# Two padding tiles ahead of and behind the normed activations of a hybrid decoder layer

## The chip, the core and the metric

The kernel runs on one core of a Trainium2 chip. The metric is the device time of one execution in microseconds (us). The time before is the median of two runs. A separate view, the profile, shows one execution instruction by instruction.

## The reference

One decoder layer on 512 tokens of width 1024, in float32, cut to what matters here:

```python
def swiglu_ffn(x, w_gate, w_up, w_down):
    return (jax.nn.silu(x @ w_gate) * (x @ w_up)) @ w_down

x = x + 0.5 * swiglu_ffn(rmsnorm(x, g1), w_gate1, w_up1, w_down1)   # 1024 -> 2816 -> 1024
x = x + mixer(rmsnorm(x, g2))       # h @ w_in (2048 columns), two causal mixers, @ w_out
x = x + 0.5 * swiglu_ffn(rmsnorm(x, g3), w_gate2, w_up2, w_down2)
y = rmsnorm(x, g4)
```

The mixer splits h @ w_in into a convolution branch (gated, depthwise convolution of width 31, layer norm, swish) and a recurrent branch (convolution of width 4, gates, a scan over the tokens, multiplied by a GELU branch).

## The kernel before

**Products in two parts.** Every large product is made from float32r operands that are split in a high and a low part: hi*hi + lo*hi + hi*lo, so three matmuls for one product. Weights come from HBM in slabs of 512 KB (`raw`). ScalarE copies the high part into `hl[:, 0]`, and VectorE (in some stages GpSimd) writes the low part into `hl[:, 1]`. `raw` has 3 buffers and `hl` has 5.

**Two kinds of matmul streams.** They differ in which operand stands still in the array and which one moves through it.

- `mm_feat` (line 194): the weights `hl` stand still, 128 columns at a time, and the normed and transposed activations `h_hi` and `h_lo` move, 512 tokens or 256 tokens at a time. It makes gate and up of both feed-forward blocks (PSUM tiles `pgate`, `pup`) and the input projection of the mixer (`pz`). 24 matmuls make one unit.
- `mm_tok` (lines 329 to 331): the inner activations (`act`, or `uhi`, `ulo`, `yhi`, `ylo` of the mixer) stand still and the weights `hl` move, always 512 columns. It makes the down products and the output projection (PSUM tiles `pd`, `pdl`).

```python
seq = [(0, h_hi), (0, h_lo), (1, h_hi)]
for s, (a, h) in enumerate(seq):
    for k in range(KT):                                  # mm_feat, KT = 8
        PE.matmul(ps, w[:, a, k, :], h[:, k, t0:t0 + n], ...)

PE.matmul(ps, ahi, whi, start=first, stop=False)          # mm_tok
PE.matmul(ps, ahi, wlo, start=False, stop=False)
PE.matmul(ps, alo, whi, start=False, stop=last)
```

The first operand after `ps` is the stationary one, the second is the moving one. Each matmul comes with a weight load of its own (PEld in the profile).

**Order of the stages**, with the times at which they stand in the profile: first norm and two early pairs of units on 256 tokens (12 to 39 us), gate and up on 512 tokens (39 to 129), first part of down (129 to 183), gate and up (183 to 318), down (318 to 364), mixer with the recurrences, the convolutions, the output projection and the first units of the second feed-forward block (364 to 609), the rest of gate and up (609 to 684, mostly on 256 tokens), down (684 to 739), gate and up (739 to 874), down and the final norm (874 to 946).

**Tiles in SBUF.** The pool `cp` holds one buffer for each persistent tile, in the order in which `const` is called (line 76). Its first tile begins 128 bytes past a multiple of 512 in each partition. The four tiles `xt0` to `xt3` take 4096 bytes each, and `h_hi` and `h_lo` 16384 bytes each. A 128-column slice of float32r is 512 bytes and a 512-column slice 2048 bytes, so all slices of one tile that the matmuls read begin at the same offset modulo 512. In the built program before, these offsets are:

| tile | role | offset modulo 512 |
|---|---|---|
| `h_hi`, `h_lo` | moving in `mm_feat` | 128 |
| `hl` (5 buffers) | stationary in `mm_feat`, moving in `mm_tok` | 480 |
| `act`, `uhi`, `ulo`, `yhi`, `ylo` (19 shared buffers) | stationary in `mm_tok` | 480 |
| `raw` (3 buffers) | source of the split | 480 |

Of the kernel before, what the change touches and what calls it, by code (L numbers as in the profile page):

```python
# [13 lines left out]
P = 128  # L14
# [44 lines left out]
def layer_kernel(ctx: ExitStack, tc, x, gains, w_g1, w_u1, w_d1a, w_d1b, w_in,  # L59
# [16 lines left out]
    def const(shape, name, dt=F32):  # L76
        return cp.tile(shape, dt, name=name, tag=name)

# [1 line left out]
    xt = [const([P, D], f"xt{t}") for t in range(4)]  # L80
    h_hi = const([P, KT, T], "h_hi", F32R)
    h_lo = const([P, KT, T], "h_lo", F32R)
    ident = const([P, P], "ident")
    ones = const([P, P], "ones")
    neghalf = const([P, 1], "neghalf")
# [16 lines left out]
        nc.sync.dma_start(g, gains[i:i + 1, :].broadcast_to([P, D]))  # L102
        return g

# [1 line left out]
    clock = {"pe": 0.0, "dve": 0.0, "pool": 0.0}  # L106
    chains, convs, done = [], [], {}

    def dve(us):
        clock["dve"] = max(clock["dve"], clock["pe"] - 3.0) + us  # L110

    # slabs are loaded, then split into two parts of float32r
    def slab_load(st, src):
        st["raw"] = wp.tile([P, D], F32, name=nm("raw"), tag="raw", bufs=RAW_BUFS)
        nc.sync.dma_start(st["raw"], src)
# [69 lines left out]
            if evac is not None:  # L185
                evac()

# [1 line left out]
    def mm_feat(ps, hl, t0, n):  # L189
        w = hl.rearrange("p s (k f) -> p s k f", k=KT)  # L190
        seq = [(0, h_hi), (0, h_lo), (1, h_hi)]
        for s, (a, h) in enumerate(seq):
            for k in range(KT):
                PE.matmul(ps, w[:, a, k, :], h[:, k, t0:t0 + n],  # L194
                          start=(s == 0 and k == 0), stop=(s == 2 and k == KT - 1))
# [5 lines left out]
            tc.keep_in_program_order(ins)  # L201
        return ins

    # a bank for the products beside the main ones
    def side_tile(name):
        if "free" in done:
            return pd.tile([P, T], F32, name=nm(name), tag="pd")
        return pp.tile([P, T], F32, name=nm(name), tag="pg")

# [1 line left out]
    def m4(name, dt=F32):  # L211
        return sp.tile([P, 4, HT], dt, name=nm(name), tag="act", bufs=ACT_BUFS)

# [58 lines left out]
        if key is not None:  # L272
            done[key] = True

# [1 line left out]
    def ffn_units(acts, j, wg, wu, parts, shared=False):  # L276
        box = {}

        def gate(t0, n, hl):
            if hl is not None:  # L280
                box["g"] = hl
            pg = pp.tile([P, T], F32, name=nm("pgate"), tag="pg")
            mm_feat(pg[:, :n], box["g"], t0, n)
            box["pg"] = pg

        def gate_out(t0, n):
            pg = box["pg"]
            sg = sp.tile([P, T], F32, name=nm("sg"), tag="sg", bufs=2)
            S.activation(sg[:, :n], pg[:, :n], AF.Silu)  # L289
            box["s"] = sg  # L290

        def up(t0, n, hl):
            if hl is not None:
                box["u"] = hl
            pu = pp.tile([P, T], F32, name=nm("pup"), tag="pg")
            mm_feat(pu[:, :n], box["u"], t0, n)
            box["pu"] = pu

        def up_out(t0, n):
            pu = box["pu"]  # L300
            sg = box["s"]
            act = acts[j]
            V.tensor_mul(sg[:, :n], pu[:, :n], sg[:, :n])  # L303
            S.copy(act[:, 0, t0:t0 + n], sg[:, :n])
            V.tensor_sub(act[:, 1, t0:t0 + n], sg[:, :n], act[:, 0, t0:t0 + n].bitcast(F32))  # L305
            dve(0.8 if n == 256 else 1.3)

        out_ = []
        for i, (t0, n) in enumerate(parts):
            us = 5.12 * n / 512  # L310
            out_.append((wg[j] if i == 0 else None, shared, us,
                         lambda hl, t0=t0, n=n: gate(t0, n, hl),
                         lambda t0=t0, n=n: gate_out(t0, n)))
            out_.append((wu[j] if i == 0 else None, shared, us,
                         lambda hl, t0=t0, n=n: up(t0, n, hl),
                         lambda t0=t0, n=n: up_out(t0, n)))
        return out_
# [6 lines left out]
            self[j] = new_act()  # L324
            return self[j]

# [1 line left out]
    def mm_tok(ps, ahi, alo, whi, wlo, first, last):  # L328
        PE.matmul(ps, ahi, whi, start=first, stop=False)  # L329
        PE.matmul(ps, ahi, wlo, start=False, stop=False)  # L330
        PE.matmul(ps, alo, whi, start=False, stop=last)  # L331
# [7 lines left out]
    def pd_tile():  # L339
        return pd.tile([P, 512], F32, name=nm("pd"), tag="pd")  # L340

    # down products of the first group of feature tiles, one half of the
    # output columns at a time, all tokens
    def down_a_units(wd, acts):
        box = {}

        def unit(oh, kp, hl):
            if kp == 0:
                box["ps"] = [pd_tile() for _ in range(4)]
            ps = box["ps"]  # L350
            hv = hl.rearrange("p s (j d) -> p s j d", j=2)
            for j in range(2):
                k = 2 * kp + j
                for t in range(4):
                    ts_ = slice(t * P, (t + 1) * P)
                    mm_tok(ps[t], acts[k][:, 0, ts_], acts[k][:, 1, ts_],
                           hv[:, 0, j, :], hv[:, 1, j, :], k == 0, k == NA - 1)

        def fin(oh):
            for t in range(4):  # L360
                add_res(t, oh, box["ps"][t], 0.5)

        return [(wd[oh, kp], False, 5.12, lambda hl, oh=oh, kp=kp: unit(oh, kp, hl),
                 (lambda oh=oh: fin(oh)) if kp == NA // 2 - 1 else None)
                for oh in range(2) for kp in range(NA // 2)]

    # products of two token tiles with the full width of the output
    def pair_units(ws, order, kept, left, toks, scale, shared, after, again=False):
        box = {}
        n = len(order)  # L370

        def unit(i, k, hl):
            if hl is None:
                hl = kept.pop(k)
            elif k in kept:
                kept[k] = hl
            if i == 0:
                done.pop("free", None)
                box["ps"] = [[pd_tile() for _ in range(2)] for _ in range(2)]
            ps = box["ps"]  # L380
            for j in range(2):
                hi, lo = left(k, j)
                for oh in range(2):
                    os_ = slice(oh * 512, (oh + 1) * 512)
                    mm_tok(ps[j][oh], hi, lo, hl[:, 0, os_], hl[:, 1, os_], i == 0, i == n - 1)

        def fin():
            for i, t in enumerate(toks):
                for oh in range(2):
                    add_res(t, oh, box["ps"][i][oh], scale)  # L390
            done["free"] = True
            after()

        return [(None if again and k in kept else ws[k], shared, 2.56,
                 lambda hl, i=i, k=k: unit(i, k, hl), fin if i == n - 1 else None)
                for i, k in enumerate(order)]
# [12 lines left out]
        order = [4, 5, 6, 7, 0, 1, 2, 3] if (YF0, YF1)[half] else list(range(8))  # L409
        return pair_units(w_out, order, {}, left, (2 * half, 2 * half + 1), 1.0, True, after)  # L410

# [1 line left out]
    def par(c, i):  # L413
        return ch[:, c, i:i + 1]

# [93 lines left out]
                    yield 0.4  # L509
        chains.append((PR_LN, layernorm(cv, half)))  # L510

    # mean over the channels, the same in every partition
    def channel_mean(v, box):
        ps2 = sp.tile([P, 2, HT], F32, name=nm("ps2"), tag="sg", bufs=2)
        V.tensor_add(ps2, v[:, 0:2, :], v[:, 2:4, :])
        V.tensor_add(ps2[:, 0, :], ps2[:, 0, :], ps2[:, 1, :])
        dve(1.1)
        for _ in range(NY3):
            yield 1
        pm = side_tile("pm")  # L520
        PE.matmul(pm[:, :HT], ones, ps2[:, 0, :], start=True, stop=True)
        box.append(pm)
# [106 lines left out]
        V.tensor_scalar_mul(psp, q, 8.0)  # L629
        V.tensor_scalar_mul(nsp, q, -8.0)  # L630

# [1 line left out]
    row1 = sp.tile([1, P], F32, name="row1", tag="sg", bufs=2)  # L633
    V.memset(row1, 1.0)
    g1ps = [pd_tile() for _ in range(2)]
# [28 lines left out]
        return lambda: chains.append(  # L664
            (PR_NORM, norm_chain(toks, gains_of[n], f"h{n}{toks[0] // 2}")))

    # the same slabs once more, for the other half of the tokens
    def again_units(first, second):
        out_ = []
        for i, (_, _, us, mm, evac, _) in enumerate(second):  # L670
            box = {}
            first[i][5]["keep"] = box
            out_.append((None, False, us, lambda hl, mm=mm, box=box: mm(box.pop("hl")), evac))
        return out_
# [48 lines left out]
    for j in range(NB):  # L723
        u += ffn_units(b2, j, w_g2[NA:], w_u2[NA:], [ALL])

    # last down products and the final norm
    last = {}

    def final(k, hl):
# [100 lines left out]
```

## Time and profile before

| what | value |
|---|---|
| median of the two runs | 949.03 us (946.58 and 951.47) |
| profiled execution, first to last instruction (span) | 945.9 us |
| busy in the span: PE, PEld, DVE, ACT, POOL | 907.8, 776.7, 475.1, 368.6, 210.8 us |
| granted TensorE clock, mean | 0.987 |
| matmuls on PE | 4796 |

The span of the profiled execution lies 3.1 us below the median of the runs. No time of its own is listed for it beside the span. The busy time of PE and PEld is the union of records whose ends are modelled and that overlap one another. So how long a matmul takes in a stream is read from the distance between starts, not from its record's duration. In the chain that ended last, a row is a start, a length and a count, and for a run of matmuls the length divided by the count is just that distance.

### The profile page before, as it was taken

Reading aid. Unit: us, or ns where it says so; the run is one execution under the profiler, and the core shown is the slowest. Engines: PE = TensorE matmul, PEld = TensorE weight load, DVE = VectorE, ACT = ScalarE, POOL = GpSimd, SP = SyncE. Lnnn points to the kernel's source line nnn. Section 1 sums busy time; section 2 is a strip of 40 time slices with the busy share of each in tenths; the row PEclk is TensorE's granted clock in tenths of the full one; section 3 lists DMA queues with packets and bytes.
Section 4 is the critical chain, followed back from the end, with each engine's and each line's share of the span. In section 5 each row is a group of like instructions: output and inputs, shape, how many; then the busy total and the mean of one; then the engine's idle time right before and its main releaser. Section 6 shows DMA issues by size and latency. Waiting matters only on the chain.

```text
span 945.9 us, 11886 instructions
## 1 busy us (share of the span) xinstructions
PE 907.8 (96%) x4796; PEld 776.7 (82%) x4796; DVE 475.1 (50%) x677; ACT 368.6 (39%) x502; POOL 210.8 (22%) x120
## 2 busy tenths in 40 slices
PE   8999999999999999988889798999999999999997
PEld 6988888888888889888878697799988888888885
DVE  6533333333333433989999897555523333333224
ACT  6522221132222334466876554644511222223113
POOL 2000000000000038884856786700000000000001
PEclk9999999999999999998999899999999999999999
DMA  8322222322222344552433444445533222232202
GB/s 273 121 90 99 101 89 93 108 89 89 89 98 103 123 167 149 186 199 99 148 130 119 153 163 150 158 174 181 184 107 111 89 89 89 94 107 89 89 24 89
DMA packets 33401, 115.94 MB, mean 123 GB/s; under 512 B 4673, under 2 KB 4801, under 8 KB 33346
## 3 DMA queue, kind: packets, MB, share of 16 engines
q1 hardware_dynamic: 32770, 114.14, 34.8%
q10 hardware_dynamic: 576, 1.05, 0.3%
q8 instruction: 37, 0.61, 0.3%
q14 instruction: 18, 0.15, 0.0%
HBM read 113.07 MB, written 2.10 MB: 122 GB/s over the span
## 4 chain that ended last, share of the span: by engine, by line
PE 82%; DVE 13%; ACT 1%; DMA 1%; POOL 1%; issue 1%; SPq 0%; POOLq 0%; ACTq 0%; DVEq 0%
PE pgate L194 25%; PE pup L194 24%; PE pd L331 8%; PE pd L329 8%; PE pd L330 8%; PE pz L194 5%; DVE pc L506 4%; DVE xr L462 2%; PE pdl L331 1%; PE pdl L330 1%; PE pdl L329 1%; DVE th L595 1%; DVE xn L226 1%; DVE act L305 1%; DMA raw<-in_w_u 1%
## 5 line engine op out<-in xcount | busy, mean ns | idle before, releaser
L119 ACT CAST hl<-raw 128x1024 fp32r<-128x1024 f32 x208 | 217.7, 1048 | 330.6 <-PE pup L194 149.5
L133 DVE TENSOR_TENSOR hl<-raw,hl 128x1024 fp32r<-128x1024 f32 x136 | 168.2, 1237 | 290.3 <-ACT hl L119 290.3
L133 POOL TENSOR_TENSOR hl<-raw,hl 128x1024 fp32r<-128x1024 f32 x72 | 180.8, 2520 | 390.6 <-ACT hl L119 385.1
L194 PE MATMUL pgate<-h_hi,hl 128*128 128x512 f32 (+1 forms) x880 | 184.6, 352 | 0.8 <-ACT h_hi L246 0.8
L194 PE MATMUL pup<-h_hi,hl 128*128 128x512 f32 (+1 forms) x880 | 184.3, 351 | 0.3 <-DVE sg L303 0.3
L194 PEld LDWEIGHTS pgate<-h_hi,hl 128*128 128x128 f32 x880 | 145.0, 190 | 25.8 <-ACT h_hi L246 1.5
L194 PEld LDWEIGHTS pup<-h_hi,hl 128*128 128x128 f32 x880 | 144.9, 190 | 24.8 <-DVE sg L303 0.5
L329 PE MATMUL pd<-hl,act 128*128 128x512 f32 x304 | 118.4, 390 | 0.0
L331 PE MATMUL pd<-hl,act 128*128 128x512 f32 x304 | 118.3, 389 | 0.0
L330 PE MATMUL pd<-hl,act 128*128 128x512 f32 x304 | 118.3, 389 | 0.0
L506 DVE SCALAR_TENSOR_TENSOR pc<-ub,ch,pc 128x256 f32<-128x256 f32 x232 | 94.6, 477 | 0.0
L194 PE MATMUL pgate<-h_lo,hl 128*128 128x512 f32 (+1 forms) x440 | 92.3, 352 | 1.8 <-DVE h_lo L252 1.8
L194 PE MATMUL pup<-h_lo,hl 128*128 128x512 f32 (+1 forms) x440 | 91.7, 350 | 0.0
L289 ACT ACTIVATE sg<-pgate 128x512 f32<-128x512 f32 (+1 forms) x55 | 28.2, 513 | 159.0 <-PE pgate L194 159.0
L194 PEld LDWEIGHTS pgate<-h_lo,hl 128*128 128x128 f32 x440 | 72.5, 190 | 14.2 <-DVE h_lo L252 2.0
L194 PEld LDWEIGHTS pup<-h_lo,hl 128*128 128x128 f32 x440 | 72.1, 188 | 12.1
L303 DVE TENSOR_TENSOR sg<-pup,sg 128x512 f32<-128x512 f32 (+1 forms) x55 | 32.0, 583 | 94.6 <-PE pup L194 94.6
L758 POOL TENSOR_SCALAR sf<-sf 128x1 f32<-128x1 f32 x4 | 1.2, 300 | 323.7 <-ACT sqo L755 323.7
L194 PE MATMUL pz<-h_hi,hl 128*128 128x256 f32 x512 | 70.4, 287 | 0.0
L331 PEld LDWEIGHTS pd<-hl,act 128*128 128x128 f32 x304 | 57.1, 188 | 11.9
L329 PEld LDWEIGHTS pd<-hl,act 128*128 128x128 f32 x304 | 57.1, 188 | 11.8
L330 PEld LDWEIGHTS pd<-hl,act 128*128 128x128 f32 x304 | 57.1, 188 | 11.7
(118 smaller groups left out, 759.9 us busy)
## 6 DMA issues: line engine op xcount, KB each, us to landing
raw<-in_w_g SPq DMA_DIRECT2D x53, 512.0 KB, 3.2
raw<-in_w_u SPq DMA_DIRECT2D x53, 512.0 KB, 3.2
raw<-in_w_in SPq DMA_DIRECT2D x32, 512.0 KB, 3.2
raw<-in_w_d1b SPq DMA_DIRECT2D x22, 512.0 KB, 3.2
raw<-in_w_out SPq DMA_DIRECT2D x16, 512.0 KB, 3.2
raw<-in_w_d2b SPq DMA_DIRECT2D x12, 512.0 KB, 3.2
raw<-in_w_d1a SPq DMA_DIRECT2D x10, 512.0 KB, 3.2
raw<-in_w_d2a SPq DMA_DIRECT2D x10, 512.0 KB, 3.2
```

The costliest lines, as they stand in the source:

```text
L119: S.copy(st["hl"][:, 0, :], st["raw"])
L133: eng.tensor_sub(st["hl"][:, 1, sl], st["raw"][:, sl], st["hl"][:, 0, sl].bitcast(F32))
L194: PE.matmul(ps, w[:, a, k, :], h[:, k, t0:t0 + n], start=(s == 0 and k == 0), stop=(s == 2 and k == KT - 1))
L226: V.scalar_tensor_tensor(out=xn, in0=xt[t], scalar=ss[:, 1:2], in1=g, op0=ALU.mult, op1=ALU.mult)
L289: S.activation(sg[:, :n], pg[:, :n], AF.Silu)
L303: V.tensor_mul(sg[:, :n], pu[:, :n], sg[:, :n])
L305: V.tensor_sub(act[:, 1, t0:t0 + n], sg[:, :n], act[:, 0, t0:t0 + n].bitcast(F32))
L329: PE.matmul(ps, ahi, whi, start=first, stop=False)
L330: PE.matmul(ps, ahi, wlo, start=False, stop=False)
L331: PE.matmul(ps, alo, whi, start=False, stop=last)
L462: V.scalar_tensor_tensor(out=xr[:, c, :], in0=rxb[:, c, half * HT + k:half * HT + k + HT], scalar=par(c, P_LW + k), in1=xr[:, c, :], op0=A ...
L506: V.scalar_tensor_tensor(out=cv[:, c, :] if j == 30 else acc, in0=src, scalar=par(c, P_DW + j), in1=acc, op0=ALU.mult, op1=ALU.add)
```

## The change

Two more tiles are put into the pool `cp`: `pad0` with 88 float32 (352 bytes a partition) ahead of `h_hi`, and `pad1` with 40 (160 bytes) behind `h_lo`. Nothing writes or reads them. `h_hi` and `h_lo` then begin at offset 480 modulo 512 instead of 128. The pads add up to 512 bytes, so all tiles behind `pad1` move by 512 bytes and keep their offset modulo 512, and the tiles ahead of `pad0` stay where they are. The built programs have the same instructions in the same order on every engine, with the same semaphores and the same PSUM banks. Only SBUF addresses and line numbers (two higher) differ. The rest of the diff removes comments.

```diff
     xt = [const([P, D], f"xt{t}") for t in range(4)]
+    const([P, 88], "pad0")
     h_hi = const([P, KT, T], "h_hi", F32R)
     h_lo = const([P, KT, T], "h_lo", F32R)
+    const([P, 40], "pad1")
     ident = const([P, P], "ident")
...
```

| tile | offset modulo 512 before | after |
|---|---|---|
| `h_hi`, `h_lo` | 128 | 480 |
| `hl`, `act`, `uhi`, `ulo`, `yhi`, `ylo`, `raw` | 480 | 480 |

## The prediction, made before the changed kernel ran

> **What bounds the kernel now.** I read the page first, its busy shares and then the chain that ended last.
>
> ```profile
> PE 907.8 (96%) x4796; PEld 776.7 (82%) x4796; DVE 475.1 (50%) x677; ACT 368.6 (39%) x502; POOL 210.8 (22%) x120
> PE 82%; DVE 13%; ACT 1%; DMA 1%; POOL 1%; issue 1%; SPq 0%; POOLq 0%; ACTq 0%; DVEq 0%
> ```
>
> TensorE is busy for 96% of the span and holds 82% of the chain. No other engine comes near, except VectorE with 13%, which lies in the mixer. So a nanosecond less between two matmuls is worth a nanosecond of the kernel wherever PE holds the chain. The question is what one matmul costs, and next came the groups of instructions by line with shapes kept apart. The number behind the bar's comma is the mean length of a record in ns.
>
> ```profile
> L194 PE MATMUL pup<-h_hi,hl 128*128 128x512 f32 x528 | 134.4, 396 | 0.0
> L194 PE MATMUL pgate<-h_hi,hl 128*128 128x512 f32 x528 | 134.4, 396 | 0.0
> L331 PE MATMUL pd<-hl,act 128*128 128x512 f32 x304 | 118.3, 389 | 0.0
> L194 PE MATMUL pgate<-h_lo,hl 128*128 128x512 f32 x264 | 67.2, 396 | 0.0
> L194 PE MATMUL pup<-h_lo,hl 128*128 128x512 f32 x264 | 67.2, 396 | 0.0
> ```
>
> Two streams of the same shape, 128x128 against 512 columns, differ: where `h` moves (line 194) a record is 396 ns, where `hl` moves (line 331) 389 ns. The idle column is 0.0 in both, so neither waits for anyone. Records overlap, so I took the true distance from the chain in order of time (start, length, what, count).
>
> ```profile
> 39.18 5.62 PE pgate L194 x24
> ...
> 123.52 5.63 PE pup L194 x24
> 183.59 5.62 PE pgate L194 x24
> ```
>
> From 39.18 to 129.15 (123.52 + 5.63) there are 16 units of 24 matmuls: 89.97 / 384 = **234.3 ns** each. From 129.15 to 183.59 there are the 240 matmuls of the first down stage: 54.44 / 240 = **226.8 ns** each. Is that the clock or the load on other engines? The stretches say no.
>
> ```profile
> 39.20:129.00 89.80, 89.80 (x385) 72.16 (x385) 29.41 (x32) 24.63 (x32) 0.00 (x0) 1.00 0.29 101
> 130.90:183.40 52.50, 52.50 (x233) 43.48 (x232) 16.76 (x18) 9.49 (x9) 0.00 (x0) 1.00 0.29 101
> ```
>
> Columns are PE, PEld, DVE, ACT, POOL, clock, DMA share and GB/s. The granted clock is 1.00 in both, DMA is the same, DVE is a third busy in both. What is left are the operands. In the faster stream both the moving and the stationary slice begin at offset 480 modulo 512; in the slower one 128 and 480, a difference of 160 bytes. The timeline just behind a change of streams tells more (start, length, engine, line, what).
>
> ```profile
> 129.69 0.39 PE L329 MATMUL pd<-hl,act 128*128 128x512 f32 x1
> 129.91 0.39 PE L330 MATMUL pd<-hl,act 128*128 128x512 f32 x1
> 130.14 0.40 PE L331 MATMUL pd<-hl,act 128*128 128x512 f32 x1
> 130.38 0.39 PE L329 MATMUL pd<-hl,act 128*128 128x512 f32 x1
> ...
> 131.07 0.39 PE L329 MATMUL pd<-hl,act 128*128 128x512 f32 x1
> 131.29 0.39 PE L330 MATMUL pd<-hl,act 128*128 128x512 f32 x1
> 131.52 0.39 PE L331 MATMUL pd<-hl,act 128*128 128x512 f32 x1
> 131.75 0.39 PE L329 MATMUL pd<-hl,act 128*128 128x512 f32 x1
> ```
>
> The down stream starts at 128.99. Its first distances are still long: 129.69 to 130.38 is 690 ns for three. From 131.07 on it is 680 ns for three, and stays so. So the same instructions at the same addresses need some ten matmuls to fall into step, as if the read of the moving slice and the load of the next stationary slice took a fixed phase to each other. The line 194 stream never falls into step in 384 matmuls. Equal offsets are a plausible condition for it.
>
> **The change, part by part.** It adds no instruction, moves none, and changes no semaphore. `pad0` sets `h` from 128 to 480; `pad1` keeps all later tiles at their old offset. The writers of `h`, ScalarE's transposed copies and VectorE's low parts, get another offset too.
>
> ```profile
> L252 DVE TENSOR_TENSOR h_lo<-ptr,h_hi 128x512 fp32r<-128x512 f32 x24 | 15.4, 680 | 6.4 <-ACT h_hi L246 6.2
> L246 ACT CAST h_hi<-ptr 128x512 fp32r<-128x512 f32 x24 | 13.0, 592 | 1.7 <-PE ptr L242 1.7
> ```
>
> They take 28.4 us in all. If the offset changed them by the 3% that part the two streams, that would be 0.9 us either way, mostly beside matmuls. I count nothing.
>
> *512 columns.* The rows above give 528 + 528 + 264 + 264 = 1584 matmuls, all in stages where PE waits for nothing. I take the distance of the down stream for them: 1584 x (234.3 - 226.8) = **11.9 us**.
>
> *256 columns.* No row shows this shape with equal offsets. The longest run of it stands in the second feed-forward block, and the first in the mixer.
>
> ```profile
> 633.78 2.81 PE pgate L194 x24
> ...
> 681.65 2.81 PE pup L194 x24
> 363.84 22.79 PE pz L194 x192
> ```
>
> (681.65 + 2.81 - 633.78) / 432 = 117.3 ns, half of 234.3 to within 0.2 ns; the mixer's 22.79 / 192 = 118.7 ns. So the price goes with the columns, and I take half of 226.8, **113.4 ns**. The bounds: a gain of nothing (117.3 stays, as a load that comes twice as often may not fall into step), and from the other side the same 7.5 ns an instruction as at 512 columns.
>
> Where PE holds the chain, this gives: 432 x 3.9 = 1.7 us at 634 to 684, and 192 x 5.3 = 1.0 us at 364 to 387. For the other places these rows of the chain count:
>
> ```profile
> 33.54 2.82 PE pgate L194 x24
> 428.81 3.78 PE pz L194 x16
> 433.67 2.85 PE pz L194 x24
> 444.76 5.64 PE pz L194 x48
> 609.42 2.85 PE pgate L194 x24
> ```
>
> The 192 early ones (12 to 39 us), at 4 to 5 ns, give 0.9 us. Between 428 and 451 the mixer has 136 (these rows and two more of 24), 0.7 us. The 96 from 609 to 622 give 0.5 us. Sum at 256 columns: **4.8 us** of 1048 matmuls, with ends of 0 and 1048 x 7.5 = 7.9 us.
>
> *The rest of the mixer.* About 776 more such matmuls lie between 386 and 609 us, where this row stands:
>
> ```profile
> 386.00:609.00 223.00, 196.41 (x1277) 179.68 (x1276) 197.75 (x331) 140.22 (x199) 161.69 (x71) 0.95 0.43 149
> 408.00:430.00 22.00, 15.88 (x127) 15.41 (x126) 21.24 (x25) 12.19 (x21) 16.39 (x10) 0.91 0.53 188
> ```
>
> VectorE works 197.8 of 223 us, and at 408 to 430 us 21.2 of 22 while PE stands still for 6. The convolution's accumulations are VectorE's, and they start when the first `pz` units are out. Faster matmuls only wait longer for them, so I count nothing; all of it on the path would be 776 x 5 = 3.9 us.
>
> *What is late next.* A unit of 5.62 us becomes 5.44, and ScalarE, VectorE and the slab loads must keep that pace. In the first quoted stretch they are busy 27%, 33% and 29%, so they do. At 256 columns a unit takes 2.72 us:
>
> ```profile
> 633.70:684.20 50.50, 50.50 (x433) 50.50 (x432) 29.31 (x36) 24.29 (x36) 0.00 (x0) 1.00 0.51 178
> ```
>
> At 58%, 48% and 51% of the time, 3% more pace doesn't make one of them the bound.
>
> *Sum:* 11.9 + 4.8 = 16.7 us. The profiled span becomes 945.9 - 16.7 = 929.2 us. The span lies 3.1 us below the median of the runs, so I set the prediction at 949.0 - 16.7 = **932.3 us**, or 1.8% less.
>
> A rule speaks against all this. The Trainium skill, "SBUF — State Buffer", section "Who interferes with whom", gives TensorE two SBUF read ports, one for the moving operand and one for the weight load, independent of each other, and says that only the pair shared by VectorE and GpSimd ever contends. By it no address relation could matter and the sum would be 0. The trace does not contradict it outright, but it leaves the 226.8 and 234.3 ns of the same shape unexplained, so I give it the chance of the first rival only.
>
> [...]
>
> **The rivals.**
>
> *No change, 949 us.* The offset isn't what parts the streams. Line 194 sends 24 matmuls into one PSUM tile and walks through eight slices of `hl` and `h`; lines 329 to 331 change the tile every three and repeat a slice. For it: no row shows `h` at another offset. Against it: within each group of three, the step that changes the PSUM tile is as long as the others (131.52 to 131.75 is 230 ns with the rounding of the rows, 131.07 to 131.29 is 220, and the sum of three is 680 throughout), so the change of tile isn't priced.
>
> *Only the wide ones fall in step, 937 us.* 949.0 - 11.9, the bound of nothing at 256 columns.
>
> *More than I count, 928 us or less.* The mixer's 3.9 us come as well (928.4), or 256 columns gain 7.5 ns each (929.2); both together give 925.
>
> *Slower, 961 us.* The streams fall into step, but at a bad phase, where each step is as long as the longest at the head of the down stream: 240 ns from 130.14 to 130.38, which is 5.7 above 234.3. At 512 columns that is 1584 x 5.7 = 9.0 us, at 256 half of it, 1048 x 2.85 = 3.0 us; 949.0 + 12.0. It decides as soon as the gate units from 39 us on take more than 5.62 us. Against it: the one stream that does fall into step does so at its shortest steps.
>
> **How the numbers follow.** Forecast (927 to 936, with the spread of the runs) 0.56; wide ones only 0.08; more than I count 0.09; no change 0.21; slower 0.06. The likeliest's own range is 927 to 936. A range that leaves out no more than 2 in 10 has to reach down to 925 and, past the wide-only case, up to no change with its highest run: 925 to 951. A measurement of this kernel can tell about 2% from no change, so 930.1 is the line. Part of the forecast's lower half and the case above it fall beyond it: faster 0.21. Slower by over 2% would need 968 us, over one and a half times the slower rival's price: 0.02. Within 2%: 0.77.
>
> **What would show it.** In the changed profile a unit of 24 in the chain should last 5.44 us instead of 5.62 at 512 columns, and 2.72 instead of 2.81 at 256; the records of the `h` rows should fall from 396 to about 389 ns; the down stage should begin at its final pace without the ten long steps; `pd` rows should stay as they are. PE's idle time in the mixer should grow by what its matmuls save there. I am wrong if the gate units stay at 5.62 us, if 256 columns stay at 2.81, or if they fall but VectorE or the slab loads appear as waits of line 194.

## The result, and the profile after

The changed kernel takes **935.85 us** (934.06 to 937.63, 2 runs), against 949.03 us before. The ratio is 0.9862 with a 95% interval of 0.9821 to 0.9904: faster by 1.4%, and less than 2%. Two more comparisons of the same distances, below, gave 0.9876 (0.9843 to 0.9909) and 0.9872 (0.9843 to 0.9901).

The chain of the changed kernel in order of time (start, length, what, count; line 194 is now 196, 331 is 333):

```profile
33.98 2.88 PE pgate L196 x24
36.86 2.88 PE pup L196 x24
39.74 5.47 PE pgate L196 x24
45.21 5.44 PE pup L196 x24
...
121.37 5.44 PE pup L196 x24
181.21 5.44 PE pgate L196 x24
...
357.11 23.03 PE pz L196 x192
```

The 16 wide units run from 39.74 to 126.81, 87.07 us instead of 89.97. A unit is 5.44 us instead of 5.62, or 226.7 ns a matmul. The first one still takes 5.47, as its stream falls into step (the distance from start to start stops changing): its first four distances are 228 to 236 ns, and the next ones 226 or 227. But the narrow units (256 tokens) got longer: 2.88 us instead of 2.82, 120.0 ns a matmul. In the mixer 192 narrow matmuls take 23.03 us instead of 22.79. The long run of narrow units says the same:

```profile
626.95 2.87 PE pgate L196 x24
629.82 2.88 PE pup L196 x24
...
675.90 2.88 PE pup L196 x24
678.78 0.23 PE pd L331
```

It is 51.83 us (626.95 to 678.78) instead of 50.68. The groups by line and form show how both kinds of record moved. The first row is the narrow one of the mixer before, the other four are after:

```profile
L194 PE MATMUL pz<-h_hi,hl 128*128 128x256 f32 x512 | 70.4, 287 | 0.0
```

```profile
L196 PE MATMUL pgate<-h_hi,hl 128*128 128x512 f32 x528 | 130.4, 389 | 0.0
L196 PE MATMUL pup<-h_hi,hl 128*128 128x512 f32 x528 | 130.4, 389 | 0.0
L333 PE MATMUL pd<-hl,act 128*128 128x512 f32 x304 | 118.3, 389 | 0.0
L196 PE MATMUL pz<-h_hi,hl 128*128 128x256 f32 x512 | 71.0, 289 | 0.0
```

The wide `h` records fell from 396 to 389 ns, the same as `pd`, which stayed. The `pz` record rose from 287 to 289 ns. Behind a wide stage, the timeline shows a down stream that is in step at once:

```profile
126.65 0.39 PE L331 MATMUL pd<-hl,act 128*128 128x512 f32 x1
126.87 0.39 PE L332 MATMUL pd<-hl,act 128*128 128x512 f32 x1
127.10 0.39 PE L333 MATMUL pd<-hl,act 128*128 128x512 f32 x1
127.33 0.39 PE L331 MATMUL pd<-hl,act 128*128 128x512 f32 x1
```

Three steps are 680 ns from the first matmul on (126.65 to 127.33). Where the span went, from the starts in the two chains:

| stretch | before, us | after, us | difference |
|---|---|---|---|
| wide gate and up, four stretches, 1584 matmuls | 89.97 + 134.94 + 11.24 + 134.94 | 87.07 + 130.56 + 10.91 + 130.56 | -11.99 |
| narrow, 12 to 39 us, 192 | 27.17 | 27.58 | +0.41 |
| narrow, first in the mixer, 192 | 22.79 | 23.03 | +0.24 |
| mixer, from there to the next gate unit | 222.79 | 222.66 | -0.13 |
| narrow, behind the mixer, 96 | 13.12 | 13.24 | +0.12 |
| narrow, second half of the tokens, 432 | 50.68 | 51.83 | +1.15 |
| all else | | | +0.2 |
| span | 945.9 | 935.9 | -10.0 |

The medians differ by 13.2 us, the two profiled spans by 10.0. The two runs before lie 4.9 us apart and those after 3.6 us, so this is no contradiction. The granted clock goes with part of it: in the comparison of e4 below, five runs of the kernel before at a mean clock of 0.989 took 944.8 to 946.9 us and six at 0.983 or 0.985 took 949.0 to 951.5, while four of the changed kernel at 0.989 took 935.0 to 935.7. A run's time lies 1.7 to 1.8 us above its span wherever both are known (937.63 and 935.9, 934.06 and 932.3). By that the profiled execution of before would be a run of some 947.7 us.

### The profile page after: what moved, and what is told of

Same layout as the page of the kernel before. It is cut to its first block, busy times and chain, and to the rows that moved or that the text cites. A ratio compares the mean times of both kernels' runs of the same rounds, so it can differ in the third digit from the quotient of the medians.

```text
span 935.9 us, 11886 instructions
## 1 busy us (share of the span) xinstructions
PE 897.9 (96%) x4796; PEld 778.1 (83%) x4796; DVE 474.9 (51%) x677; ACT 368.6 (39%) x502; POOL 211.0 (23%) x120
## 4 chain that ended last, share of the span: by engine, by line
PE 82%; DVE 12%; DMA 2%; issue 1%; ACT 1%; POOL 1%; SPq 0%; POOLq 0%; ACTq 0%; DVEq 0%
PE pgate L196 24%; PE pup L196 24%; PE pd L333 8%; PE pd L331 8%; PE pd L332 8%; PE pz L196 6%; DVE pc L508 4%; DVE xr L464 2%; PE pdl L333 1%; PE pdl L331 1%; PE pdl L332 1%; PE ptr L244 1%; DVE xn L228 1%; DMA raw<-in_w_u 1%; DVE ps L518 1%
## 5 line engine op out<-in xcount | busy, mean ns | idle before, releaser
L196 PE MATMUL pgate<-h_hi,hl 128*128 128x512 f32 (+1 forms) x880 | 181.4, 348 | 0.9 <-ACT h_hi L248 0.9
L196 PE MATMUL pup<-h_hi,hl 128*128 128x512 f32 (+1 forms) x880 | 181.2, 348 | 0.8 <-DVE sg L305 0.8
L332 PE MATMUL pd<-hl,act 128*128 128x512 f32 x304 | 118.3, 389 | 0.0
L333 PE MATMUL pd<-hl,act 128*128 128x512 f32 x304 | 118.3, 389 | 0.0
L333 PEld LDWEIGHTS pd<-hl,act 128*128 128x128 f32 x304 | 57.1, 188 | 11.9
L196 PEld LDWEIGHTS pz<-h_hi,hl 128*128 128x128 f32 x512 | 66.6, 196 | 0.4
L332 PEld LDWEIGHTS pd<-hl,act 128*128 128x128 f32 x304 | 57.1, 188 | 11.7
```

Source lines behind the costliest of these rows:

```text
L196: PE.matmul(ps, w[:, a, k, :], h[:, k, t0:t0 + n], start=(s == 0 and k == 0), stop=(s == 2 and k == KT - 1))
```

## The experiments

"Distance" is here the offset of the moving slice less that of the stationary slice, in bytes. Theory: this distance sets the time of a float32r matmul.

**One pad alone.** The change has two pads, so either can be dropped. Both tests change absolute offsets, and only the second one changes the distance.

```diff
+    const([P, 88], "pad0")      # e1: this line alone
+    const([P, 40], "pad1")      # e2: this line alone
```

> Only the front pad of 352 bytes is kept. h moves to 480 modulo 512, as in the change, but everything behind it moves by 352 too, so hl and act begin at 320: the distance from the stationary slice to the moving slice is 160, as before, at other absolute offsets. Theory (the distance counts): the gate unit is back at 5.62 us, 256 columns at 117.3 to 118.7 ns, the down units stay at 226.7 ns, and the time is that of before, 949 us, ratio 1.000 within 0.4%. Rival (the absolute offset of the moving slice counts, and 480 is the good one): gate units of 5.44 us, 256 columns at 120 ns, and 936 us, ratio 0.986.

> Only the rear pad of 160 bytes is kept. h stays at 128 modulo 512, and hl and act move from 480 to 128: distance 0, as in the change, at other absolute offsets. Theory (the distance counts): 5.44 us a gate unit, 120 ns at 256 columns, 936 us, ratio 0.986. Rival (the absolute offset of h counts): 5.62 us, 117.3 ns and 949 us, ratio 1.000.

The front pad alone: 947.97 us, ratio 0.9994 (0.9977 to 1.0011), span 945.0. The rear pad alone: 935.76 us, ratio 0.9876 (0.9843 to 0.9909), span 933.1. The chains, first with the front pad alone, then with the rear pad alone:

```profile
43.09 5.63 PE pup L195 x24
48.72 5.62 PE pgate L195 x24
```

```profile
43.56 5.44 PE pup L195 x24
49.00 5.44 PE pgate L195 x24
```

With `h` at 480 and `hl` at 320 the unit is 5.62 us; with both at 128 it is 5.44. So it is the distance that counts here, and not the absolute offset. The rear pad alone is enough, and the front pad alone brings nothing. The long run of narrow units follows the distance too: 50.69 us with the front pad alone, 51.84 with the rear pad alone (50.68 before, 51.83 after).

**All distances, without the layer.** One stationary tile and 16 moving tiles, 32 bytes further on each; 40 matmuls for each tile and width.

```python
for j in range(40):
    PE.matmul(ps[:, :n], w[:, j % 8, :], mv[i][:, :n], start=(j == 0), stop=(j == 39))
```

> TensorE alone: 40 matmuls with one stationary tile (eight slices of 128 float32r columns in turn) for each of 16 moving tiles, which begin 0, 32, 64 ... 480 bytes further on than the stationary one modulo 512, with 512, 384 and 256 columns each. It leaves out all of the layer. Theory (a fixed price for each weight load where the distance is 0): from 226.7 ns at 512 and 120.0 at 256 columns follow 0.417 ns a column and 13.3 ns a matmul, so 173.3 ns at 384; at 160 it falls into no step and shows 234.3 and 117.3 to 118.7 ns. Other distances: unknown; if only meeting reads cost anything, some distance should come near 213.3 and 106.7 ns. Rival 1 (distance 0 is the best there is): no distance is below 226.7 at 512 columns. Rival 2 (the price goes with the columns and something else in the layer held 256 columns at 120 ns): 113.4 ns at 256 and distance 0. Rival 3 (it isn't the distance but the order in which slices and PSUM tiles are walked): all distances alike.

Mean distance between starts in ns, from the 11th matmul of each stream on:

| distance, bytes | 0 | 32 | 64 | 96 | 128 | 160 | 192 | 224 |
|---|---|---|---|---|---|---|---|---|
| 512 columns | 226.7 | 233.4 | 228.8 | 233.2 | 232.2 | 234.2 | 233.4 | 233.3 |
| 384 columns | 173.3 | 176.6 | 173.3 | 176.7 | 175.6 | 173.3 | 174.8 | 173.3 |
| 256 columns | 120.0 | 117.7 | 117.8 | 120.1 | 118.8 | 118.7 | 117.8 | 118.3 |

The distances 256 to 480 give these values once more, each within 0.1 ns: the period is 256 bytes, not 512. Each value is that of one stream; e8 below shows that its start can matter too. The groups by form show it in the length of the records:

```profile
L39 PE MATMUL ps<-o160b,w 128*128 128x512 f32 x40 | 9.5, 396 | 0.0
L39 PE MATMUL ps<-o256b,w 128*128 128x512 f32 x40 | 9.2, 389 | 0.0
L39 PE MATMUL ps<-o160b,w 128*128 128x256 f32 x40 | 4.9, 281 | 0.0
L39 PE MATMUL ps<-o256b,w 128*128 128x256 f32 x40 | 5.0, 283 | 0.0
```

The numbers of the layer come back in a stream that has nothing but matmuls: 234.2 and 118.7 ns at 160, 226.7 and 120.0 at 0. So rival 3 (the order in which slices and banks are walked) and rival 2 (the layer holds the narrow ones) fall. At distance 0 the three widths give 13.3 ns above 0.417 ns a column. No distance came near 213.3, and distance 0 is the best for 512 columns, as rival 1 said.

**The change again, and two other layouts**, all in one comparison. e4 is the change. In e5 the narrow units' weights begin 64 bytes further on in their buffers (five constants and the softplus scratch tiles are packed, to make room for larger `hl` buffers, which also makes the pads needless). In e6 the pads let `h` begin 64 bytes further on than `hl` for all matmuls of line 196.

```diff
-        st["hl"] = wp.tile([P, 2, D], F32R, name=nm("hl"), tag="hl", bufs=HL_BUFS)
+        flat = wp.tile([P, 2 * D + 64], F32R, name=nm("hl"), tag="hl", bufs=HL_BUFS)
+        o = SHIFT if shift else 0                    # e5: 16 floats for units of 256 tokens
+        st["hl"] = flat[:, o:o + 2 * D].rearrange("p (s d) -> p s d", s=2)
...
-    const([P, 88], "pad0")
+    const([P, 104], "pad0")                          # e6
-    const([P, 40], "pad1")
+    const([P, 24], "pad1")
```

> The changed kernel once more, in more rounds, as the yardstick of the two variants beside it. By the profiles (1584 matmuls of 512 columns at 226.7 instead of 234.3 ns, 12.0 us less; 1048 of 256 columns on the path at 120.0 instead of 117.3 to 118.7, 2.1 us more) the gain is 9.9 us and the ratio to the kernel before 0.9895. If something beside TensorE's distances gained as well, it is nearer to 0.986.

> Distance 0 for all matmuls of 512 columns and 192 modulo 256 (hl begins 64 bytes further on) for all of 256 columns: hl gets 256 bytes more a buffer, and weights whose units have 256 tokens are put 64 bytes into their buffer. To make room, five small constants share one tile and the five scratch tiles of softplus another, which also brings h to hl's offset without pads. Theory (the 256-column matmuls are what the change loses, and the distance alone sets them): gate and up of 256 tokens at 2.83 us a unit (117.8 ns) instead of 2.88, 512 columns unchanged at 5.44, and 2.3 us (1048 x 2.2 ns) less than the changed kernel: span some 933, ratio to the changed kernel 0.9975. Rival (256 columns in the layer are held by something else, such as the slabs' preparation): 2.88 us stay and the time is the changed kernel's.

> The pads are 416 and 96 bytes instead of 352 and 160: h lies 64 bytes further on than hl modulo 256 for all its matmuls. Theory (the periods of the stream of matmuls alone carry over): 228.8 ns at 512 columns, 5.49 us a unit, and 117.8 at 256, 2.83 us a unit; against the changed kernel 1584 x 2.1 = 3.3 us more and 1048 x 2.2 = 2.3 us less, so 1.0 us slower, ratio to it 1.001. Rival (only distance 0 gains): 234 ns and the time before.

| kernel | median, us | ratio to before, 95% interval | span | wide unit | narrow unit, second half |
|---|---|---|---|---|---|
| e4, the change | 935.58 | 0.9872 (0.9843 to 0.9901) | 933.9 | 5.44 | 2.88 |
| e5, narrow units 64 off | 934.73 | 0.9859 (0.9831 to 0.9886) | 933.0 | 5.44 | 2.83 |
| e6, all 64 off | 939.02 | 0.9898 (0.9872 to 0.9925) | 939.8 | 5.49 | 2.83 |

Chains of e4, e5 and e6 at the narrow units of the second half:

```profile
627.85 2.88 PE pup L196 x24
```

```profile
627.90 2.83 PE pup L196 x24
```

```profile
624.97 5.49 PE pup L196 x24
630.47 2.83 PE pgate L196 x24
```

Each of these units has the length that the bare stream gave for its distance (24 x 117.8 = 2.83, 24 x 228.8 = 5.49). So the price is the distance's here too. But the distance is not all: in e5 the last two narrow units ahead of the first wide one take 2.72 us, or 113.3 ns a matmul, at the same distance as those of 2.83, and e6 has such units in the mixer.

```profile
32.13 2.72 PE pgate L196 x24
34.85 2.72 PE pup L196 x24
```

The totals followed less well. e4 was expected 9.9 us under the kernel before (0.9895). Its median is 13.4 us under it, and the interval holds both; at the equal clock of 0.989 the medians lie 10.7 us apart. e5 was expected 2.3 us under the change and is 0.9 us under it, well inside the intervals. In the profiles its narrow units in the long run save 0.9 us (18 x 0.05) and the first 192 in the mixer 0.4 (22.61 instead of 23.03 us), but the rest of the mixer takes 0.8 us more (223.59 instead of 222.75). e5 has the lowest median of all kernels run, but that it beats the change is not shown. e6 was expected 1.0 us over the change and is 3.4 us over it, also within the intervals. In the profiles its wide stretches take 3.5 us more and these two narrow ones 1.4 less, near the forecast; another 3.8 us lie ahead of the wide units and in the rest of the mixer.

**Finer distances, smaller loads.**

> TensorE alone again, 40 matmuls for each moving tile, at 0, 4, 8, 16, 48, 64, 80, 112, 144, 176, 192, 208 and 240 bytes from the stationary slices modulo 256, with 512 and 256 columns; then at distance 0 with 64 and with 32 stationary columns instead of 128. It leaves out all of the layer. Theory (a load of 128 columns costs a fixed 13.3 ns at distance 0, by the bytes that it reads): 64 stationary columns give 6.7 ns, so 220.0 and 113.3 ns at 512 and 256 columns, and 32 give 216.7 and 110.0. Rival (the price is one of each load whatever its size): 226.7 and 120.0 stay. For the distances: if 16 bytes are the grain, 4 and 8 are as 0 (226.7 and 120.0), and odd multiples of 16 are a case of their own; none is expected below 226.7 at 512 columns.

| distance, bytes | 0 | 4 | 8 | 16 | 48 | 64 | 80 | 112 | 144 | 176 | 192 | 208 | 240 |
|---|---|---|---|---|---|---|---|---|---|---|---|---|---|
| 512 columns | 226.7 | 236.7 | 233.3 | 231.6 | 230.0 | 229.0 | 231.2 | 231.3 | 233.3 | 233.3 | 233.3 | 234.6 | 233.3 |
| 256 columns | 120.0 | 123.3 | 120.0 | 116.8 | 118.3 | 117.8 | 118.4 | 113.3 | 118.6 | 119.3 | 113.3 | 119.3 | 117.0 |

Nothing lies below 226.7 at 512 columns. At 256 two distances gave 113.3, one of them 192, which had given 117.8 in e3. The grain is finer than 16 bytes: at 512 columns neither 4 nor 8 behaves like 0, at 256 columns 4 doesn't. With 64 stationary columns at distance 0 it is 230.2 and 113.3 ns, with 32 columns 231.7 and 113.3. The theory of a price by the bytes of a load had 220.0 and 113.3, then 216.7 and 110.0. It hit one of four (113.3 with 64 columns): at 512 columns a smaller load is even slower, as the stream no longer falls into step. This theory of the mechanism fell, and so did its rival (226.7 and 120.0).

**Different starting phases, and bf16.** A short matmul of 64 to 100 columns ahead of each stream lets it start at another phase.

> TensorE alone, 40 matmuls in a stream, and ahead of each stream one short matmul of 64 to 100 columns, so that eight streams of a kind start at eight phases: 512 columns at distance 0 and at 160, 256 columns at distance 0 and at 192. Then bf16 operands at distances 0, 160 and 192 with 512 and 256 columns. It leaves out all of the layer. Theory (at distance 0 the stream always falls into the same step; at other distances it depends on the start which of several steps or cycles it takes): all eight streams at distance 0 end at 226.7 and 120.0 ns; at 160 none ends at 226.7; at 192 with 256 columns some end at 113.3 and some at 117.8 ns, which both were seen. Rival (the step depends on the distance alone): the eight streams of a kind are alike, and the 113.3 ns at 192 had another cause. bf16: if what costs is the bytes of load and stream meeting, half the bytes give at most 220.0 and 113.3 ns, and the distance changes little; if each load has its price, 226.7 and 120.0.

At distance 0 all eight streams of 512 columns end at 226.7 ns and all eight of 256 at 120.0, within the first 13 matmuls of each. At 160, none of the eight falls into step (234.1 to 234.4). At 192 and 256 columns, six end at 117.8 and two at 113.3. So the theory held, and its rival, that the distance alone decides, fell. The timeline, for 40 matmuls each (start, length):

```profile
26.00 9.34 PE L50 MATMUL ps<-o000b,w 128*128 128x512 f32 x40
53.62 9.31 PE L50 MATMUL ps<-o000b,w 128*128 128x512 f32 x40
99.90 9.61 PE L50 MATMUL ps<-o160b,w 128*128 128x512 f32 x40
224.73 4.95 PE L50 MATMUL ps<-o192b,w 128*128 128x256 f32 x40
229.56 4.79 PE L50 MATMUL ps<-o192b,w 128*128 128x256 f32 x40
243.90 8.80 PE L50 MATMUL ps<-h000b,w16b 128*128 128x512 bf16 x40
257.22 8.80 PE L50 MATMUL ps<-h160b,w16b 128*128 128x512 bf16 x40
270.55 8.80 PE L50 MATMUL ps<-h192b,w16b 128*128 128x512 bf16 x40
```

The rows at 192 are the same matmuls at the same distance, 4.95 and 4.79 us: the start decided. With bf16 operands these three distances make no difference: 215.8 ns at all of them with 512 columns, and 109.2 with 256, both under the most that the theory had for half the bytes (220.0 and 113.3).

The Trainium skill, "TensorE: Matmul & The Clock Gate", section "Back-to-back issue gap", gives N/2.4 + 2.5 ns for a warm matmul by itself, 215.8 and 109.2 ns as an estimate by that formula, and some 131 ns at 512 columns for a sustained stream of loads and matmuls. The bf16 streams here agree with the first figure, and no stream here came near the second. The float32r streams with 128 stationary columns take 4% to 13% more than the first.

## Why the prediction was right, and where not

**The bound** was read rightly: PE's distance between matmuls. Nothing else became late. VectorE's and the slabs' work kept the pace, and the mixer, set at nothing, changed by 0.13 us. PE's idle time there, which was to grow, went from 26.6 to 26.2 us (222.79 - 196.20 busy before, 222.66 - 196.47 after); its narrow matmuls had not become faster. The writers of `h`, also set at nothing, kept their 592 and 680 ns.

**512 columns:** 11.9 us forecast, 11.99 measured in the four stretches. The reading that carried it was the comparison of two streams of one shape with equal clock and load, and the ten matmuls in which the down stream fell into step. The signs that were named for them came: 5.44 us a unit, records of 389 ns, `pd` rows as they were, and a down stage that starts in step. The falling into step has moved to the first gate unit (5.47). That the distance between moving and stationary slice is the cause, and not another difference between the two lines, is shown by e1, e2 and e3.

**256 columns:** a gain of 4.8 us forecast, a loss of 1.9 us in the stretches of the table; a unit was to last 2.72 us and lasts 2.88. This term had the wrong sign. The step that failed is "the price goes with the columns, and I take half of 226.8". That 117.3 ns is half of 234.3 does not show a price by the column. Both are means of cycles out of step: at 256 columns the distances of the second half before repeat after five matmuls (115 to 120 ns), and in the mixer a stream of the same shape at the same distance goes through another cycle, with a mean of 118.7. At distance 0 the stream in step pays 13.3 ns a matmul at any width of the three. At 512 columns this is less than the mean out of step (21.0 above 213.3), at 256 more (10.6 above 106.7). The end of the range on this side, "a gain of nothing", did not go far enough. The rival of a bad phase was told for all matmuls together; only the narrow ones got slower, by 1.3 to 2.7 ns each. A narrow stream at 113.3 ns does exist, but at other distances than the change has (112 and 192 bytes in e7, 192 in e5, 64 in the mixer of e6).

**The sum:** 16.7 us forecast; 12.0 - 1.9 leaves 10.1, and the profiled spans differ by 10.0, the medians by 13.2. 935.85 lies 3.5 us above the predicted 932.3 and at the upper end of the likeliest range; the case "only the wide ones fall in step", 937 us, was nearer in its account. That the total came so near is in part luck: the median of before lies above its profiled execution by 3.1 us, more than the 1.7 to 1.8 us between a run and its span, and at an equal clock of 0.989 the gain in e4's comparison is 10.7 us. The wrong term made the forecast of the gain 6.7 us too large (4.8 + 1.9).

**No change,** the rival of the two independent read ports (the Trainium skill, "SBUF — State Buffer", section "Who interferes with whom"), fell for float32r: where the stationary and the moving slice lie to each other changes a matmul by up to 10 ns at 512 columns (226.7 to 236.7). For bf16 the runs agree with it at the three distances tried.

What stays open is why. That the two reads meet would fit a dependence on their distance modulo 256 bytes and on the phase, but it is not shown: a price by bytes was tried and fell, and no run looks into the memory itself.

## What to carry to other kernels

Compare two streams of one shape in the same profile by the distance between starts; where they differ with the clock, the load and the waits alike, look at where their operands lie, and move one of them in a test, as e1 and e2 do. For float32r streams of 512 columns that are bound by TensorE, put the moving and stationary slices at the same offset modulo 256 bytes, which here costs 160 bytes of padding a partition and is worth 3% of those matmuls (226.7 instead of 234.3 ns). For 256 columns the same offset is a poor choice (120.0 ns, against 117.8 or 113.3 at 64 and 192 bytes), though e5, which keeps them apart there, has not shown a gain in the total. Don't scale a time that holds at a fixed phase from one width to another, and measure each width by itself.

## What the runs showed of the hardware that was not expected

- A float32r stream has states: in step, its distance is constant or nearly so; out of step, it goes through a cycle. The constant ones seen are 226.7, 233.3, 173.3, 120.0 and 113.3 ns, which are 34, 35, 26, 18 and 17 times 6.67 ns, the time of 16 columns at 0.417 ns each.
- The same matmuls at the same distance can end in different states: 117.8 or 113.3 ns at 192 bytes with 256 columns, by the phase at which the stream starts.
- A smaller stationary slice can make a stream slower: 230.2 ns with 64 columns against 226.7 with 128, at distance 0 and 512 moving columns.
- The bf16 streams tried show none of this: 215.8 and 109.2 ns at distances 0, 160 and 192.
